# First two column-pair blocks of an up projection worked on form by form, with weight rings in the branches' memory and part of the sums on POOL

## The chip, the cores and the metric

The kernel runs on one core of a Trainium2 chip. The metric is the device time of one execution in microseconds (us), taken as the median of several runs. Engines are named as in the profile: PE is TensorE's matmuls and PEld its weight loads, DVE is VectorE, ACT is ScalarE, POOL is GpSimd, SP is the engine whose queue issues all DMAs of this kernel.

## The reference

One layer of a decoder trunk with two request groups: a prompt of 1024 tokens and 64 sample tokens (8 sequences of 8). All data is float32, the model width is 1024.

```python
mod = jax.nn.silu(c) @ p['w_ada'] + p['b_ada']
sh1, sc1, gt1, sh2, sc2, gt2 = jnp.split(mod, 6, axis=-1)
...
x = x + gt1[:, None] * (merged @ p['w_out'])
h = modulate(x, p['g_norm2'], sh2, sc2)
up = h @ p['w_up']
uc, new_ffn_conv = causal_dwconv(ffn_conv, up, p['ffn_conv_w'], p['ffn_conv_b'])
ua, ub = jnp.split(uc, 2, axis=-1)
x = x + gt2[:, None] * ((jax.nn.gelu(ua) * ub) @ p['w_down'])
```

Ahead of this stand a recurrent branch and a state-space branch ("the branches") that give `merged`; behind it a last norm. `modulate` is an RMS norm with a scale and a shift per channel that come from `mod`. `w_up` has 1024 rows and 6144 columns.

## The kernel before, in words

**Halves.** Activations lie with channels on the 128 partitions and tokens in columns. Tokens are cut into two halves: half 0 holds the 64 samples and 512 prompt tokens (576 columns), half 1 the other 512 prompt tokens. Float32 products are made from split operands: a value is rounded to the matmul's input format (`hi`, on ACT), the remainder `lo` is subtracted on DVE, and hi x hi, hi x lo and lo x hi are summed in PSUM. So every weight tile costs an ACT copy and a DVE subtraction (`wsplit` L167, `split_to` L240) before TensorE can use it.

**Stages.** `part1` (L1024) does the branches of one half, ending in the GLU strips and `merged`; `w_out` (L1106) does the output projection with the residual and adds up the squares of the new residual in `acc2`. Half 0 goes first. `h2a` (L1164), which turns half 0 into normalised forms, runs between the strips of half 1's GLU stage. Behind half 1's `w_out` the norm's reciprocal root `rB2` is made (`rstd_from` L349: a float32 matmul with ones, ACT root, DVE reciprocal), the pools of the branches are closed, new pools `forms` and `up` are opened, and `h2b` (L1189) and `up` (L1329) follow. Two down projections end the program.

**The modulation** `mod` is made in chunks of 512 columns: `adaB` (L1516) works on chunks 6 to 11 with split weights, eight pairs of matmuls (L269, L270) each, a few at every tick of the branches' strips of half 1.

**The up projection** treats the two halves of the tokens and two groups of weight columns as a 2 x 2 block product and uses seven products in place of eight (a Strassen-Winograd scheme). For each of 24 blocks of `w_up` four weight quarters A11, A12, A21, A22 are loaded (`quarters` L1242), and S1 = A21 + A22, S2 = S1 - A11, S3 = A11 - A21, S4 = A12 - S2 are made on DVE in place of the plain quarters. The activation side has seven "forms", made once, each in four tiles j = 0 to 3: B11 and B21 are half 0's; B22 is half 1's odd channel blocks, and with B12 its even ones, T1 = B12 - B11, T2 = B22 - T1, T3 = B22 - B12, T4 = B21 - T2. B11 and B21 come from `h2a`, the others from `h2b`. `prod` (L1225) is one product: four tiles of a form by three split terms; kinds "w" (two halves of 288 columns, 24 matmuls), "e" (512 columns, 12 matmuls) and "p" (two of 256, 24 matmuls).

`quad` (L1272) does one block in the order B11, [T4 of the block before], T1, T2, B21, B22, T3, and leaves T4 for the next block. It holds three PSUM tiles `b`, `e`, `a` of the ring `mm` (three buffers). Partial results are copied out by ACT (L1280, L1287, L1291) into the ring `cp` of four buffers, and `evac` (L1337) adds them on DVE into tiles of the ring `rx` of four. When both halves of a column tile are there, `finish` (L1353) runs the causal convolution: small copies on POOL (`fix` L1306), a scaled copy on ACT (L1320), two multiply-adds on DVE (L1322) for each half.

`h2b` loads half 1's residual (`x2B`, from DRAM, ring `rx`), multiplies by `rB2` on DVE (L1186), scales and shifts on ACT (L1187), loads half 0's raw values `hA` back (even blocks in ring `gl`, odd ones `C` in ring `cp`), makes the sums on DVE (L1207, L1212, L1213, L1217) and splits each tile (`split_form`: ACT L1147, DVE L1148).

**Order.** The program is written in one thread; a list scheduler lays it out per engine by priority, which is program order unless a `high_priority` block lifts it. Each engine, and SP's queue of DMAs, then runs its instructions strictly in that order. A tile of a ring is written only after its previous user has finished.

Of the kernel before, what the change touches and what calls it, by code (L numbers as in the profile page):

```python
# [8 lines left out]
F32 = mybir.dt.float32  # L9
# [42 lines left out]
def _body(ctx, nc, tc, a):  # L52
# [11 lines left out]
    wp, tp, ph = pool("w", 2), pool("tmp", 2), pool("part1")  # L64
    two = False
# [290 lines left out]
    def rstd_of(pr, name, tag="rstd", out=None):  # L356
        n = pr.shape[1]
        sd = rg("sd")[:, :n]
# [336 lines left out]
    us16 = ph.tile([128, 16, 16], F32, name="us16")  # L695
    ys16 = ph.tile([128, 16, 16], F32, name="ys16")
# [327 lines left out]
    def part1(half, L, X, during_glu, ahead=None):  # L1024
# [36 lines left out]
        drain(s5g)  # L1061
        during_glu()
# [43 lines left out]
    def w_out(half, merged):  # L1106
        acc2 = new_acc(f"acc2{half}")
# [76 lines left out]
    def norm_raw(dst, x, rstd, kb, t=None):  # L1184
        t = rg("nt")[:, :512] if t is None else t
        V.tensor_mul(t, x, rstd)  # L1186
        S.activation(dst, t, AF.Identity, scale=gmod["g2"][:, kb, 0:1], bias=modT[:, 24 + kb, 0:1])  # L1187

    def h2b():  # L1189

        def load(k, tag, w, n):
            t = tmp(tag, [128, w], n, bufs=4)[:, :576]
            nc.sync.dma_start(t, h2d[k])
            return t

        def nb2(dst, k):
            t = tmp("rx", [128, 656], "x2B", bufs=4)[:, :512]
            nc.sync.dma_start(t, x2d[1][k * 128:(k + 1) * 128])
            norm_raw(dst, t, rB2, k, tmp("xc", [128, 632], "nt", bufs=3)[:, :512])

        A, ST, C = [], [], []
# [12 lines left out]
        for j in range(4):  # L1214
            C.append(load(2 * j + 1, "cp", 576, "hA2"))
            split_form(form("T2", j), A[j])
            V.tensor_sub(C[j], C[j], A[j])  # L1217
        for j in range(4):
            split_form(form("B22", j), ST[j][:, 1])
        for j in range(4):  # L1220
            split_form(form("T3", j), ST[j][:, 0])
        for j in range(4):
            split_form(form("T4", j), C[j])

    def prod(acc, kind, wt, n, start=False, stop=False):  # L1225
        hi, lo = [x.rearrange("p (j c) -> p j c", c=128) for x in wt]
        for j in range(4):
            X = F[n, j]
            for i, (y, r) in enumerate(((hi, 0), (hi, 1), (lo, 0))):
                f = dict(start=start and j + i == 0, stop=stop and j == 3 and i == 2, skip_group_check=True)  # L1230
                w, x = y[:, j], X[:, r]
                if kind == "e":
                    T_.matmul(acc[:, 0], w, x, **f)  # L1233
# [8 lines left out]
    def quarters(w):  # L1242

        def new(n):
            return tmp("wr", [128, 512], n, bufs=WR)

        def load(q):
            t = new(f"wr{q}")
            nc.sync.dma_start(t, w[q])
            return t  # L1250

        def out(x):
            with tc.high_priority(offset=300):
                hi = tmp("wh", [128, 512], "wh", F32R, bufs=3)
                lo = tmp("wl", [128, 512], "wl", F32R, bufs=3)
                split_to(hi, lo, x)
            return hi, lo

        with tc.high_priority(offset=300):
            a11, a21, a22 = load(0), load(2), load(3)  # L1260
            s1 = new("s1")
            V.tensor_add(s1, a21, a22)
            s2 = new("s2")
            V.tensor_sub(s2, s1, a11)
            V.tensor_sub(a21, a11, a21)
            a12 = load(1)
            s4 = new("s4")
            V.tensor_sub(s4, a12, s2)
# [426 lines left out]
```

## Time and profile before

| | |
|---|---|
| median of 3 runs | 1776.75 us (1776.21 to 1778.32) |
| profiled execution | 1774.74 us |
| its span, first to last instruction | 1773.0 us |
| mean granted TensorE clock | 0.983 |
| instructions | 29389 |
| PE, PEld busy | 1693.0 us, 1533.8 us |
| DVE, ACT, POOL busy | 1243.4 us, 919.0 us, 187.3 us |

Times in a profile count from the first instruction. A granted clock of 1.00 is TensorE's higher level (2.4 GHz), 0.50 the lower (1.2 GHz). A wait row names the waiting engine, tile and line, and what released it.

### The profile page before, as it was taken

The page shows a single profiled execution, that of the slowest core. Times are in us where ns is not written, and L with a number is a line of the kernel's source. Part 1 is how long each engine was busy: PE and PEld are TensorE (multiplying, and loading weights), DVE is VectorE, ACT ScalarE, POOL GpSimd, SP SyncE. Part 2 cuts the span into 40 slices and gives each one's busy share as a digit, 9 for nine tenths or more (in the row PEclk, how much of TensorE's full clock was granted, in tenths as well). Part 3 has the DMA queues.
Part 4 walks back from the last instruction along what each step waited for, and adds up shares of the span by engine and source line. Part 5 has one row for each costly group of instructions (what it writes and reads, how often), then busy time and mean ns, then how long its engine had stood idle before and what let it go on. Part 6 is the DMA issues. An engine that isn't in the chain of part 4 may idle for free.

```text
span 1773.0 us, 29389 instructions
## 1 busy us (share of the span) xinstructions
PE 1693.0 (95%) x10538; PEld 1533.8 (87%) x10538; DVE 1243.4 (70%) x2645; ACT 919.0 (52%) x1616; POOL 187.3 (11%) x480
## 2 busy tenths in 40 slices
PE   7999999999999999999957999999999979999997
PEld 3899999899997877788746999999999978999887
DVE  8878688967746787756767777777777755435426
ACT  4657668435534588845445555545555435224224
POOL 0012110100000001000000222222222220000000
PEclk9999999999999999999978999999999999999999
DMA  8275344466646665446661222222222228546634
GB/s 308 74 236 168 99 119 127 126 187 194 205 125 203 213 182 153 151 125 193 196 205 32 78 76 77 80 79 75 79 75 79 73 64 289 166 130 191 197 95 136
DMA packets 151891, 250.87 MB, mean 142 GB/s; under 512 B 34112, under 2 KB 43328, under 8 KB 151744
## 3 DMA queue, kind: packets, MB, share of 16 engines
q1 hardware_dynamic: 151744, 248.99, 45.7%
q8 instruction: 83, 1.36, 0.3%
q14 instruction: 64, 0.52, 0.1%
HBM read 205.20 MB, written 43.73 MB: 140 GB/s over the span
## 4 chain that ended last, share of the span: by engine, by line
PE 65%; DVE 4%; DMA 4%; ACT 2%; issue 1%; POOL 0%; POOLq 0%; SPq 0%; DVEq 0%; ACTq 0%
PE mm L222 16%; PE b L1237 13%; PE mm L220 9%; PE e L1233 7%; PE mm L1415 7%; PE a L1237 4%; PE b L1240 4%; DMA al<-act 2%; PE pg L957 1%; DMA xB<-x 1%; PE sada L270 1%; PE sada L269 1%; DMA tgb<-tg 0%; DVE wlo L175 0%; PE sx L713 0%
## 5 line engine op out<-in xcount | busy, mean ns | idle before, releaser
L174 ACT ACTIVATE whi<-raw 128x512 fp32r<-128x512 f32 x310 | 194.5, 628 | 320.6 <-PE mm L222 104.5
L175 DVE TENSOR_TENSOR wlo<-raw,whi 128x512 fp32r<-128x512 f32 x310 | 213.1, 688 | 207.0 <-ACT whi L174 180.6
L220 PE MATMUL mm<-h1A,whi 128*128 128x288 f32 x1024 | 184.5, 299 | 0.0
L222 PE MATMUL mm<-h1B,whi 128*128 128x512 f32 x512 | 160.2, 393 | 0.0
L220 PEld LDWEIGHTS mm<-h1A,whi 128*128 128x128 f32 x1024 | 152.3, 190 | 0.2
L1237 PE MATMUL b<-T,wh 128*128 128x288 f32 x768 | 134.9, 298 | 14.5 <-ACT t L1280 13.2
L1237 PEld LDWEIGHTS b<-T,wh 128*128 128x128 f32 x768 | 115.7, 190 | 17.0 <-ACT t L1280 13.4
L241 ACT ACTIVATE wh<-wr 128x512 fp32r<-128x512 f32 x96 | 60.5, 630 | 113.8 <-PE b L1237 43.0
L222 PEld LDWEIGHTS mm<-h1B,whi 128*128 128x128 f32 x512 | 95.5, 188 | 23.7
L220 PE MATMUL mm<-h1A,wlo 128*128 128x288 f32 x512 | 111.0, 298 | 2.0 <-DVE wlo L175 2.0
L222 PE MATMUL mm<-h1B,wlo 128*128 128x512 f32 x256 | 100.7, 393 | 0.7 <-DVE wlo L175 0.7
L1322 DVE SCALAR_TENSOR_TENSOR uc<-up,vec,uc 128x624 f32<-128x624 f32 (+1 forms) x96 | 76.2, 815 | 30.6 <-ACT uc L1320 29.5
L1322 DVE SCALAR_TENSOR_TENSOR gl<-up,vec,gl 128x624 f32<-128x624 f32 (+1 forms) x96 | 75.5, 807 | 28.4 <-ACT gl L1320 27.6
L220 PE MATMUL mm<-act,whi 128*128 128x288 f32 x512 | 90.3, 297 | 1.6 <-ACT act L1147 1.1
L242 DVE TENSOR_TENSOR wl<-wr,wh 128x512 fp32r<-128x512 f32 x96 | 65.9, 686 | 34.7 <-ACT wh L241 34.2
L220 PEld LDWEIGHTS mm<-h1A,wlo 128*128 128x128 f32 x512 | 83.1, 190 | 2.3 <-DVE wlo L175 2.3
L1237 PE MATMUL b<-B,wh 128*128 128x288 f32 x384 | 68.3, 300 | 16.1 <-ACT wh L241 16.1
L1237 PE MATMUL b<-T,wl 128*128 128x288 f32 x384 | 82.9, 297 | 0.0
L1415 PE MATMUL mm<-act,whi 128*128 128x512 f32 (+1 forms) x304 | 82.7, 359 | 0.0
L220 PEld LDWEIGHTS mm<-act,whi 128*128 128x128 f32 x512 | 75.5, 189 | 2.8 <-DVE act L1148 1.4
L1237 PEld LDWEIGHTS b<-B,wh 128*128 128x128 f32 x384 | 57.6, 193 | 16.9 <-ACT wh L241 16.9
L241 ACT ACTIVATE wh<-s 128x512 fp32r<-128x512 f32 x72 | 45.0, 625 | 50.9 <-PE b L1237 42.6
(441 smaller groups left out, 4347.7 us busy)
## 6 DMA issues: line engine op xcount, KB each, us to landing
raw<-w_in SPq DMA_DIRECT2D x128, 256.0 KB, 2.8
raw<-w_down SPq DMA_DIRECT2D x105, 256.0 KB, 2.8
wr<-w_up SPq DMA_DIRECT2D x96, 256.0 KB, 2.7
raw<-w_ada SPq DMA_DIRECT2D x64, 256.0 KB, 3.0
act<-uc SPq DMA_DIRECT2D x48, 256.0 KB, 2.1
araw<-w_ada SPq DMA_DIRECT2D x16, 512.0 KB, 7.4
s5a<-s5d SPq DMA_DIRECT2D x16, 512.0 KB, 4.0
raw<-w_rgp SPq DMA_DIRECT2D x32, 256.0 KB, 2.7
```

What stands on the lines that cost most here:

```text
L174: S.activation(hi, raw, AF.Copy)
L175: V.tensor_sub(lo, raw, hi.bitcast(F32))
L220: T_.matmul(T[m][:, h, :288], y[:, k, c], x[:, r, h * 288:(h + 1) * 288], **f)
L222: T_.matmul(T[0][:, m, tok], y[:, k, c], x[:, r, tok], **f)
L241: S.activation(hi, src, AF.Copy)
L242: V.tensor_sub(lo, src, hi.bitcast(F32))
L269: T_.matmul(sa[:18], csr[:, kb], hi, start=kb == 0, stop=False)
L1233: T_.matmul(acc[:, 0], w, x, **f)
L1237: T_.matmul(acc[:, h, :288], w, x[:, h * 288:(h + 1) * 288], **f)
L1240: T_.matmul(acc[:, h, o:o + 256], w, x[:, h * 256:(h + 1) * 256], **f)
L1322: V.scalar_tensor_tensor(dst, t[:, k:k + n], fw[:, k, m:m + 1], dst, op0=OP.mult, op1=OP.add)
L1415: T_.matmul(T[:, m, tok], y[:, k, c], act[kb][:, r, tok], start=kb + n == 0, stop=kb == 23 and n == 2, skip_group_check=True)
```

## The change

It touches four things.

*Memory.* The tiles of the branches that are done early go into a pool `branches` on the other side of SBUF; `lead_weights`, called in `part1` of half 1 after the state-space branch has been drained and ahead of the GLU strips, closes it and puts the rings `wr`, `wh`, `wl` of the up projection's weights there. It loads the first block's four quarters at once and makes their sums on POOL.

*The norm.* The last two squares of `w_out` are not added by DVE; the norm's matmul takes three tiles. `rB2` is made inside `up_lead`.

*The forms.* `h2b` makes B22 first, then T1, T2, T3, T4. The subtractions of T3 and T4 go to POOL (`G`). T4 is made in `hA`'s own tile; the odd blocks come in the ring `xc` of three, as does the residual; the ring `cp` is left alone.

*The lead.* For the first two blocks (`w_up[0]` and `w_up[12]`, the two parts of one column pair) the products go form by form. The last modulation chunk is taken out of `adaB` and made behind the norm's matmul from float32 operands without a split. From the third block on the order is that of before. T1's product is now added on top of B22's in one PSUM tile for these two blocks, so their T3 evacuation has a subtraction and an addition.

```diff
+    early = ctx.enter_context(ExitStack())
+    rp = early.enter_context(tc.tile_pool(name="branches", bufs=1, side="right"))
+    RIGHT = ("s5", "yT", "gw", "us16", "ys16")
...
-        return ph.tile(shape, dt, tag=tag, name=name, bufs=bufs)
+        return (rp if tag.startswith(RIGHT) else ph).tile(shape, dt, tag=tag, name=name, bufs=bufs)
...
-        return tp.tile(shape, dt, tag=tag, name=name, bufs=bufs)
+        return (rp if rp is not None and tag in ("xc", "h") else tp).tile(shape, dt, tag=tag, name=name, bufs=bufs)
...
         drain(s5g)
+        if not smp:
+            lead_weights()
         during_glu()
...
-                acc_sq(acc2, xo, m == 0)
+                if half == 1 and b == 3:
+                    last.append(rg("sq")[:, :512])
+                    S.activation(last[-1], xo, AF.Square)
+                else:
+                    acc_sq(acc2, xo, m == 0)
...
-        return acc2
+        return [acc2, *last]
...
         def nb2(dst, k):
-            t = tmp("rx", [128, 656], "x2B", bufs=4)[:, :512]
+            t = tmp("xc", [128, 632], "x2B", bufs=3)[:, :512]
             nc.sync.dma_start(t, x2d[1][k * 128:(k + 1) * 128])
...
         for j in range(4):
-            A.append(load(2 * j, "gl", 632, "hA1"))
             ST.append(slot512(4 + j, f"h2B{j}"))
+            nb2(ST[j][:, 1], 2 * j + 1)
+            split_form(form("B22", j), ST[j][:, 1])
+        for j in range(4):
+            A.append(load("gl", 2 * j, 4))
+        for j in range(4):
             nb2(ST[j][:, 0], 2 * j)
-            t = tmp("wr", [128, 512], "t1f", bufs=WR)
-            V.tensor_sub(t, ST[j][:, 0], A[j][:, 32:544])
-            split_form(form("T1", j), t)
+            V.tensor_sub(A[j][:, 32:544], ST[j][:, 0], A[j][:, 32:544])
+            split_form(form("T1", j), A[j][:, 32:544])
+            G.tensor_sub(ST[j][:, 0], ST[j][:, 1], ST[j][:, 0])
         for j in range(4):
-            t3, b22 = ST[j][:, 0], ST[j][:, 1]
-            nb2(b22, 2 * j + 1)
-            V.tensor_sub(t3, b22, t3)
-            V.tensor_add(A[j][:, 32:544], t3, A[j][:, 32:544])
+            V.tensor_sub(A[j][:, 32:544], ST[j][:, 1], A[j][:, 32:544])
+            split_form(form("T2", j), A[j])
         for j in range(4):
-            C.append(load(2 * j + 1, "cp", 576, "hA2"))
-            split_form(form("T2", j), A[j])
-            V.tensor_sub(C[j], C[j], A[j])
-        for j in range(4):
-            split_form(form("B22", j), ST[j][:, 1])
+            c = load("xc", 2 * j + 1, 3)
+            G.tensor_sub(A[j], c, A[j])
         for j in range(4):
             split_form(form("T3", j), ST[j][:, 0])
         for j in range(4):
-            split_form(form("T4", j), C[j])
+            split_form(form("T4", j), A[j])
...
+        def sums(self, eng):
+            t = self.t
+            t["S1"] = wt("wr", "S1", F32, WR)
+            eng.tensor_add(t["S1"], t["A21"], t["A22"])
+            t["S2"] = wt("wr", "S2", F32, WR)
+            eng.tensor_sub(t["S2"], t["S1"], t["A11"])
+            eng.tensor_sub(t["A21"], t["A11"], t["A21"])
+            t["S3"] = t.pop("A21")
+            t["S4"] = wt("wr", "S4", F32, WR)
+            eng.tensor_sub(t["S4"], t["A12"], t["S2"])
...
+    def lead_weights():
+        nonlocal rp, uw
+        early.close()
+        rp = None
+        uw = early.enter_context(tc.tile_pool(name="upw", bufs=1, side="right", reuse_waits="tile"))
+        lead.append(Blocks(a["w_up"][0]))
+        lead[0].load("A11", "A21", "A22", "A12")
+        lead[0].sums(G)
...
+                elif e is not None:
+                    V.tensor_sub(o, y, z)
+                    V.tensor_add(o, o, e)
...
+    def up_lead():
+        nonlocal rB2
+        gl = {}
+        Q = [Quad(q, evac_up(0, i, gl)) for i, q in enumerate(lead)]
+        for i in range(2):
+            if i == 1:
+                x = slot512(2, "wx")
+                Q.append(Quad(Blocks(a["w_up"][12], (("A11", x[:, 0]), ("A12", x[:, 1]))), evac_up(0, 1, gl)))
+                Q[1].q.load("A11", "A12")
+            Q[i].p1()
+            Q[i].p2()
+        rB2 = slot(3, "rstdB2", F32)[:, 0, :512]
+        rstd_from(acc2, 512, "rstdB2", out=rB2)
+        e = mm("e")
+        ada_tail()
+        h2b()
+        Q[0].p3_first(e[:, 0])
+        with tc.high_priority(offset=300):
+            Q[1].q.load("A21", "A22")
+            Q[1].q.sums(G)
+        Q[1].p3_first(e[:, 1])
+        for q in Q:
+            q.p5_last()
+        Q[0].p6()
+        Q[0].c12()
+        Q[0].p7()
+        Q[0].p4()
+        Q[1].p6()
+        Q[1].c12()
+        Q[1].p7()
+        return Q[1]
+
+    def ada_tail():
+        sa = psum("ms", [128, 512], "sada")
+        for kp in range(4):
+            x = one(f"T3_{kp}", [128, 2, 512], "araw", F32)
+            nc.sync.dma_start(x, a["w_ada"][kp * 256:(kp + 1) * 256, 3584:4096].rearrange("(k p) c -> p k c", p=128))
+            for k in range(2):
+                T_.matmul(sa[:18], cs[:, 2 * kp + k], x[:, k], start=kp + k == 0, stop=kp + k == 4)
+        t = tmp("xc", [128, 632], "adat", bufs=3)
+        S.activation(t[:18, :512], sa[:18], AF.Copy)
+        ada_fin(44, 4, t)
...
-    adaB = ada_gen((6, 7, 8, 9, 10, 11), lambda: mm("sada")[:, 0],
+    adaB = ada_gen((6, 7, 8, 9, 10), lambda: mm("sada")[:, 0],
```

In the methods of `Quad`, p1 is the product of A11 with B11, p2 of A12 with B21, p3 of S4 with B22, p5 of S1 with T1, p6 of S2 with T2, p7 of S3 with T3, p4 of A22 with T4; `c12` is the evacuation that p3 and p5 end in.

## Rows read from the trace of the kernel before

**Rows 1.** First part of the page: busy us, share of the span, instructions

```profile
PE 1693.0 (95%) x10538; PEld 1533.8 (87%) x10538; DVE 1243.4 (70%) x2645; ACT 919.0 (52%) x1616; POOL 187.3 (11%) x480
```

**Rows 2.** Windows: us, busy of PE, PEld, DVE, ACT, POOL, PEclk, DMA share, GB/s

```profile
904.60:924.90 20.30, 1.21 (x4) 0.32 (x3) 16.84 (x23) 11.91 (x18) 0.46 (x1) 0.60 0.82 262
924.90:936.30 11.40, 11.40 (x60) 10.44 (x60) 11.40 (x19) 8.40 (x15) 0.00 (x0) 0.82 0.44 154
936.30:949.50 13.20, 0.03 (x2) 0.01 (x1) 12.85 (x22) 4.80 (x9) 0.00 (x0) 0.61 0.08 20
949.50:960.00 10.50, 10.50 (x61) 9.96 (x62) 6.64 (x10) 5.98 (x9) 2.18 (x8) 0.83 0.14 29
960.00:981.20 21.20, 21.20 (x146) 20.12 (x145) 14.33 (x22) 11.38 (x18) 2.96 (x12) 1.00 0.17 49
```

**Rows 3.** Waits of TensorE, 880 to 965: us in total, times, longest

```profile
PE b L1237 <- ACT wh L241: 16.1, 1, 16.1
PE b L1237 <- ACT t L1280: 13.2, 1, 13.2
```

**Rows 4.** The chain that ended last, products: start us, us, engine, tile, line

```profile
924.88 5.46 PE b L1237 x24
...
972.53 3.20 PE a L1237 x24
975.73 2.79 PE e L1233 x12
978.52 2.84 PE b L1240 x24
```

**Rows 5.** A window of the branches (columns as in 2), readers of tile h

```profile
772.00:800.00 28.00, 28.00 (x126) 23.17 (x125) 10.67 (x17) 7.52 (x13) 0.00 (x0) 1.00 0.48 139
...
L1006 DVE TENSOR_TENSOR gy<-gy,h x16: 666/686/693, 212.1 to 771.5; 128x512 f32<-128x512 f32 x16
```

**Rows 6.** Timeline of a chunk's pair, its window, fp32 matmuls at the start

```profile
736.18 0.39 PE L269 MATMUL sada<-adahl,csr 128*18 128x512 f32 x1
736.40 0.39 PE L270 MATMUL sada<-adahl,csr 128*18 128x512 f32 x1
...
720.00:740.00 20.00, 20.00 (x91) 15.23 (x90) 16.71 (x27) 17.80 (x31) 0.00 (x0) 1.00 0.58 184
...
19.77 3.63 PE L305 MATMUL sada<-araw,cs 128*18 128x256 f32 x16
```

**Rows 7.** Timeline of the norm's chain: start us, us, engine, line, operation

```profile
908.85 0.69 ACT L359 ACTIVATE sd<-prs,epst 128x512 f32<-128x512 f32 x1 [0.76 <-PE prs L353]
909.57 3.35 DVE L364 RECIPROCAL rstdB<-sd 128x512 f32<-128x512 f32 x1 [1.98 <-ACT sd L359]
...
913.68 0.81 ACT L1187 ACTIVATE h2B<-nt,modT,gm_g 128x512 f32<-128x512 f32 x1 [4.15 <-DVE nt L1186]
...
915.25 0.63 ACT L1147 ACTIVATE T<-t1f 128x512 fp32r<-128x512 f32 x1 [0.76 <-DVE t1f L1207]
```

**Rows 8.** VectorE while the forms are made: window, timeline, group

```profile
912.90:951.50 38.60, 13.45 (x68) 12.48 (x69) 36.89 (x60) 22.43 (x36) 1.14 (x2) 0.63 0.42 135
...
943.18 2.49 DVE L1148 TENSOR_TENSOR B<-h2B,B 128x512 fp32r<-128x512 f32 x4
...
L1217 DVE TENSOR_TENSOR hA<-hA,hA 128x576 f32<-128x576 f32 x4 | 3.0, 751 | 0.0
```

**Rows 9.** POOL beside VectorE: per line ns min/median/max, then timeline

```profile
L1369 DVE TENSOR_TENSOR uc<-uc,gl x48: 675/684/692, 981.7 to 1458.8; 128x512 f32<-128x512 f32 x48
...
L1367 POOL TENSOR_TENSOR cs<-uc,gl x24: 832/1317/1969, 981.3 to 1457.7; 128x64 f32<-128x64 f32 x24
...
1206.42 0.82 DVE L1322 SCALAR_TENSOR_TENSOR uc<-up,vec,uc 128x512 f32<-128x512 f32 x1
...
1238.30 0.74 DVE L1322 SCALAR_TENSOR_TENSOR uc<-up,vec,uc 128x512 f32<-128x512 f32 x1
```

**Rows 10.** VectorE in the GLU stage, timeline

```profile
843.97 0.69 DVE L1079 SCALAR_TENSOR_TENSOR q<-tgb,q 128x512 f32<-128x512 f32 x1 [2.96 <-DMA tgb<-tg]
```

More of the change, by code (lines that the diff above doesn't have):

```diff
@@ L694, in _body @@
     quarter = const.tile([128, 1], F32, name="quarter")
-    us16 = ph.tile([128, 16, 16], F32, name="us16")
-    ys16 = ph.tile([128, 16, 16], F32, name="ys16")
+    us16 = one("us16", [128, 16, 16], "us16")
+    ys16 = one("ys16", [128, 16, 16], "ys16")
     x2d = [dp.tile([1024, 512], F32, name=f"x2d{h}") for h in range(2)]
@@ L1106, in w_out @@
     def w_out(half, merged):
-        acc2 = new_acc(f"acc2{half}")
+        acc2, last = new_acc(f"acc2{half}"), []
         for b in range(4):
@@ L1240, in prod, with __init__, load, take @@
                             T_.matmul(acc[:, h, o:o + 256], w, x[:, h * 256:(h + 1) * 256], **f)
[L1242 to L1252, printed above, removed]
+    class Blocks:
+        def __init__(self, w, own=()):
+            self.w, self.t = w, dict(own)
+        def load(self, *names):
+            for n in names:
+                t = self.t.setdefault(n, None)
+                if t is None:
+                    t = self.t[n] = wt("wr", f"w{n}", F32, WR)
+                nc.sync.dma_start(t, self.w[{"A11": 0, "A12": 1, "A21": 2, "A22": 3}[n]])
+        def sums(self, eng):
[8 more added lines that the diff above has]
+            eng.tensor_sub(t["S4"], t["A12"], t["S2"])
+        def take(self, n):
@@ new lines, in blocks_of, with product, __init__, cp @@
+            q.load("A11", "A21", "A22", "A12")
+            q.sums(V)
+        return q
+    def product(q, acc, kind, n, x, **f):
+        prod(acc, kind, q.take(n), x, **f)
+    class Quad:
+        def __init__(self, q, evac):
+            self.q, self.evac, self.p3_ = q, evac, None
+        def cp(self, dst, src):
+            with tc.high_priority(offset=400):
+                S.activation(dst, src, AF.Copy)
+        def p1(self):
+            self.b = mm("b")
+            product(self.q, self.b, "w", "A11", "B11", start=True, stop=True)
+            self.t1 = tmp("cp", [128, 576], "t1", bufs=4)
+            self.cp(halves(self.t1), self.b[:, :, :288])
+        def p2(self):
+            a_ = mm("a")
+            product(self.q, a_, "w", "A12", "B21", start=True, stop=True)
+            self.evac(0, 0, a_[:, :, :288], halves(self.t1))
+        def p3_first(self, e):
+            self.e = e
+            product(self.q, e, "e", "S4", "B22", start=True, stop=True)
+            self.p3_ = tmp("cp", [128, 576], "p3", bufs=4)[:, :512]
+            self.cp(self.p3_, e)
+        def p5_last(self):
+            product(self.q, self.e, "e", "S1", "T1", stop=True)
+        def c12(self):
+            self.evac(0, 1, self.e, self.u2)
+        def p5(self):
+            self.e = mm("e")[:, 0]
+            product(self.q, self.e, "e", "S1", "T1", start=True, stop=True)
+            self.p5_ = tmp("cp", [128, 576], "p5", bufs=4)[:, :512]
+            self.cp(self.p5_, self.e)
+        def p6(self):
+            product(self.q, self.b, "w", "S2", "T2", stop=True)
+            self.u2 = tmp("cp", [128, 576], "u2", bufs=4)[:, :512]
+            self.cp(halves(self.u2), pmid(self.b))
+        def p3(self):
+            product(self.q, self.e, "e", "S4", "B22", stop=True)
+            self.c12()
+        def p7(self):
+            product(self.q, self.b, "p", "S3", "T3", stop=True)
+            if self.p3_ is None:
+                self.evac(1, 1, pmid(self.b), halves(self.p5_))
+            else:
+                self.evac(1, 1, pmid(self.b), halves(self.p3_), halves(self.e))
+        def p4(self):
+            product(self.q, self.b, "w", "A22", "T4", stop=True)
+            self.evac(1, 0, self.b[:, :, :288], None)
@@ L1351, in up @@
-        pend()
+                q = Quad(blocks_of(a["w_up"][12 * part + b]), evac_up(b, part, gl))
+                q.p1()
+                pend.p4()
+                q.p5()
+                q.p6()
+                q.p2()
+                q.p3()
+                q.p7()
+                pend = q
+        pend.p4()
     def finish(i, raw, part, m, gl, k):
@@ L1533, in _body @@
     tp = pool("up", 2)
-    h2b()
+    rB2 = None
     up()
@@ L1538, in _body @@
     phase.close()
+    early.close()
     pairs.close()
```

107 lines of the change are left out of this document (34 added, 73 removed).

## The prediction

> **What bounds the kernel now.** The page's first part says TensorE: it is busy 95% of the span, no other engine over 70% [rows 1]. So a change pays where TensorE stands idle or where it takes matmuls off TensorE. The windows around the start of the up projection show where that is [rows 2]: from the end of the second half's output projection (904.6 us) TensorE works 1.21 us of 20.30, then a burst of 11.40, then nothing for 13.20; only from 949.5 on is it busy without a break. The granted clock column shows 0.82 and 0.83 in the two bursts that follow the idle stretches, so part of each burst ran at the lower of its two levels (1.2 instead of 2.4 GHz).
>
> The waits name the two reasons [rows 3]. 16.1 us: the first product waits for the split of its first weight block, whose load is issued only after the new pools have opened. 13.2 us: the next product on the same PSUM tile waits for ScalarE's copy L1280; that copy needs a buffer of the ring `cp`, and `h2b` holds all four for its tiles `C` until T4 is split.
>
> Thirteen products (all seven of the first block, six of the second, up to its T3 product) end at 981.2, so they take 76.6 us from 904.6. At the high clock a product of 24 matmuls takes 3.20, an "e" product 2.79, a T3 product 2.84; the first product after the idle stretch took 5.46 [rows 4]. Work is therefore 7 x 3.20 + 4 x 2.79 + 2 x 2.84 = 39.2 us; 37 us of the 76.6 are waiting and low clock.
>
> **The change part by part.**
>
> *The lead.* Four products need only the first half's forms, which exist already: 4 x 3.20 = 12.8, so 904.6 to 917.4 if the weights are there. The first block's four loads and sums move into memory that the branches leave. In program order they stand before the GLU stage, and the last reader of that memory starts at 771.5. I let them run in 772 to 800, where VectorE is busy 10.67 of 28 us and DMA share is 0.48 [rows 5]: cost nothing; if that cover is gone they fall into the GLU stage (fourth rival). The second block's two loads wait for one merged tile that the output projection reads until its last strip, and land under the first two products, 6.4 us.
>
> *The norm.* Its matmul now sums three tiles and stands behind the four products. A 256-column fp32 record takes 3.63 / 16 = 0.227 [rows 6]; a 512-column fp32 matmul is two records of twice that, 0.91, so three take 2.7: 920.1. The two additions on VectorE that go (2 x 0.60) no longer lie on the path. Then, by the durations of the chain now [rows 7]: root 0.69, reciprocal 3.35, and with 0.1 for hand-over 924.2; multiply, shift and round 0.60 + 0.81 + 0.63: first B22 form at 926.2.
>
> *The modulation chunk.* Sixteen matmuls at 0.22 [rows 6] leave a stretch of the branches in which TensorE is busy 20.00 of 20 us [rows 6]: 16 x 0.22 = 3.5 us gained. Eight fp32 matmuls come back behind the norm, 8 x 0.91 = 7.3, from 920.1 to 927.4, under the chain of the norm, so free. Their four loads of 512 KB stand on SP's queue ahead of the residual's; 2 MB at the 262 GB/s of that window [rows 2] is 8 us, with the first three residual tiles 10.7 of the 19.6 us between 904.6 and 924.2, so hidden. The ring `xc` has three tiles, so later loads wait in SP's queue for a tile, and the loads behind them wait too; I take nothing, with 2 us as the bad end.
>
> *Forms.* From 924.2 VectorE is the engine to count: in the same work now it is busy 36.89 of 38.60 us [rows 8]. Back to back, 512 columns take (2.49 - 0.68) / 3 = 0.60, 576 columns about 0.67 [rows 8]. After: 28 operations of 512 columns (8 norm products; 4 each of T1's subtraction, T1's low part, T2's subtraction, B22's and T3's low parts) and 8 of 576 (the low parts of T2 and T4): 16.8 + 5.4 = 22.2. Added to that 8 weight splits (4.8), 5 evacuations (3.0, with the new extra subtraction in it) and about 8 convolution steps of finished tiles at 0.75 (6.0): 36.0, and 1.7 of bubbles as now: 961.9. One T3 product after that, 2.84: the thirteenth product ends at 964.7. TensorE alone would allow 904.6 + 39.2 + 2.7 + 7.3 = 953.8. So without contention 981.2 - 964.7 = 16.5 us are gained.
>
> *POOL.* The trace has no two-input POOL operation of 512 columns. Sixteen come: four in the branches, four early (second block, while VectorE waits for the norm) and eight beside the forms. What they cost VectorE is bounded so. From below nothing: 48 VectorE operations L1369 run next to POOL's 64-column multiplication and all take 675 to 692 ns [rows 9]. From above: POOL shuts VectorE out for all of its time. The 64-column operation lasts 832 to 1969 ns, median 1317 [rows 9]; for 512 columns 0.8 us (if length did not matter) to 10.5 (eight times the median). I take the nearest row: one VectorE operation that starts under that multiplication took 0.82 where its like takes 0.74 [rows 9], 0.08 more; times eight for the columns is 0.64, times eight operations 5.1 us on the path. The Trainium skill, page "SBUF — State Buffer", section "SBUF: two separate sides", says otherwise: a VectorE operation with two SBUF inputs and a reading POOL operation hold one port pair in turn, each for its whole length, the other stopped. By that rule the sum is -9.5 instead of -14.9 (second rival).
>
> *What queues behind.* POOL's sums stand ahead of the small copies of the first finished tiles; ScalarE's convolution copy waits for those, and through the ring `rx` the next evacuations: one or two sums, at most 2.6 us at 1.32, taken as nothing because VectorE's 36 us already fill that time. TensorE's bursts after 927 may run at the low level; a product then costs up to the 5.46 - 3.20 = 2.3 us seen now [rows 4], hidden while VectorE sets the pace, 2 us more if it is the last one.
>
> *The rest.* The other eleven column pairs run the same products in the same order; they are busy without a break now and stay so: nothing.
>
> **Sum.** -3.5 - 16.5 + 5.1 = -14.9 against the profiled execution's own 1774.74 (span 1773.0 and 1.7 around it): 1759.8. That execution lies 2.0 below the median of the runs, 1776.75, so the forecast is 1761.8, taken as 1762.
>
> **The rivals.** Differences under 0.2% (3.6 us) cannot be told from none here.
>
> 1. *Forecast*, 0.58: 1762; its own range 1756 to 1767.
>
> 2. *The port shuts VectorE out*, 0.14. Each of the eight POOL sums beside the forms stops it for a median 1.32: 8 x 1.32 = 10.5 instead of 5.1. -20.0 + 10.5 = -9.5: 1767. For it: nearly all of VectorE's work there has two SBUF inputs, and POOL's 64-column operations are stretched beside it. Against: the unstretched L1369. The Trainium skill, page "GPSIMD Engine Reference", section "3. Performance versus the Vector engine", gives 4497 ns for 2048 columns, by which one sum is an estimated 1.1 us and the eight 9.0; no run here shows it yet.
>
> 3. *Slower: POOL becomes the bound of the forms*, 0.08. T3 and T4 cannot be split before POOL has subtracted, and POOL takes them one by one. It decides when a sum costs the path more than 2.9 us: -20.0 + 8 x 2.95 = +3.6. At the upper bound, 10.5 each, it is +64: 1841; at 3.5 each it is +8: 1785. For it: the stretch to 1969 ns at 64 columns. Against: POOL stands idle otherwise, and VectorE waiting for it leaves it the port.
>
> 4. *The early work disturbs the GLU stage*, 0.09. There VectorE already waits 2.96 us for a DMA [rows 10]. If the 1 MB of weights or the POOL sums fall there, about that wait and its low-clock tail again, 5 us: 1767.
>
> 5. *TensorE-bound lead*, 0.08. If the norm's matmul is put ahead of the lead, as soon as the squares are there (907), VectorE starts 10 us earlier and 953.8 is reached: -27.4 - 3.5: 1746.
>
> 6. *It does not do what it says*, 0.03. If the early weights still wait for a tile that is released late, the first product waits its 16 us as now, and only the `cp` wait goes, mostly eaten by POOL: within 0.2%.
>
> **How the numbers follow.** Range 1749 to 1773: below it most of the fifth case, above it the third and sixth and the worse ends of the second and fourth. Faster by over 0.2%: cases 1, 2, 4, 5 less 0.03 for their bad ends, 0.86. Within: 0.06. Slower: 0.08.
>
> **What would show it.** In the profile after: no idle TensorE between 904 and 917 at granted clock 1.00; the chunk's fp32 matmuls before the first "e" product; no wait for the `cp` copy; VectorE nearly full from 924 to 960; the thirteenth product ending some 65 us after the output projection (964.7 + 5.1 - 904.6). VectorE operations of 512 columns at a pitch of over 1 us beside POOL's would show the second rival, TensorE waiting long on a split that waits for POOL the third. A gap in the GLU stage wider than now shows the fourth. I am wrong if the stretch from 904.6 to the thirteenth product stays over 73 us.

## The result and the profile after

The kernel after the change takes 1767.01 us (median, 1765.94 to 1769.02), the one before 1777.53 in the same session: a ratio of 0.9943, 95% interval 0.9925 to 0.9960. The forecast was 1762 us, a gain of 14.9 us; 10.5 were gained. (Ratios here and below are of undisturbed executions alone; in E11 the profiled one took 5095.7 us and is left out.)

"The stretch" below runs from the end of the second half's output projection to the end of the thirteenth product. The page's first part, the windows of the stretch (us, busy of PE, PEld, DVE, ACT, POOL, PEclk, DMA share, GB/s) and TensorE's waits from 895 to 972, which answer to [rows 1 to 3]:

```profile
PE 1707.3 (97%) x10542; PEld 1536.3 (87%) x10542; DVE 1246.5 (71%) x2621; ACT 913.9 (52%) x1608; POOL 228.6 (13%) x496
```

```profile
900.06:916.40 16.34, 15.57 (x103) 13.65 (x103) 6.02 (x7) 6.53 (x10) 2.68 (x8) 1.00 0.36 120
916.40:928.07 11.67, 7.42 (x22) 1.76 (x21) 5.24 (x9) 3.10 (x6) 1.14 (x4) 0.94 0.80 276
928.07:950.00 21.93, 15.86 (x45) 10.50 (x46) 20.64 (x25) 15.14 (x25) 8.75 (x6) 0.73 0.47 135
950.00:971.95 21.95, 20.12 (x127) 18.06 (x126) 21.95 (x30) 11.30 (x18) 6.17 (x8) 0.91 0.12 37
```

```profile
PE e L1242 <- DVE T L1158: 4.2, 3, 1.7
PE e L1242 <- ACT B L1157: 3.6, 1, 3.6
PE e L1242 <- ACT p L1302: 1.9, 2, 1.0
```

The waits of 16.1 and 13.2 us are gone. The lead runs at clock 1.00, as forecast; then come a second window in which VectorE is busy only 5.24 of 11.67 us, and two in which VectorE is full and TensorE's mean clock is 0.73 and 0.91. The output projection ends at 900.06, the thirteenth product, in the chain of work that ended last (start, us, engine, tile, line), at 971.95:

```profile
961.21 2.16 PE b L1249 x16
963.37 4.28 PE b L1246 x32
...
968.84 3.10 PE b L1249 x24
971.95 6.40 PE b L1246 x48
```

That is 71.9 us where the kernel before took 76.7 and the forecast was 65. From there to the down projection's start the two agree (483.1 and 483.2 us). Two places took the missing 7 us. First, the timelines of VectorE, ScalarE and TensorE around the norm's root (start, us, engine, line, operation, idle before it and what ended it):

```profile
914.63 3.35 DVE L368 RECIPROCAL rstdB<-rstdB 128x512 f32<-128x512 f32 x1 [1.78 <-ACT rstdB L363]
...
924.52 0.20 DVE L330 TENSOR_TENSOR modT<-adap,vec 128x36 f32<-128x36 f32 x1 [5.34 <-PE adap L328]
924.75 0.19 DVE L331 TENSOR_TENSOR modT<-modT,adap 128x36 f32<-128x36 f32 x1
925.25 1.34 DVE L1195 TENSOR_TENSOR x2B<-x2B,rstdB 128x512 f32<-128x512 f32 x2 [0.30 <-DMA x2B<-x2d]
```

```profile
912.61 1.28 ACT L363 ACT_TABLE_LOAD   x1
...
916.35 7.04 PE L1450 MATMUL sada<-araw,cs 128*18 128x512 f32 x16
924.07 0.42 PE L328 MATMUL adap<-vec,adat 18*128 18x18 f32 x4 [0.68 <-ACT adat L1452]
928.07 1.52 PE L1242 MATMUL e<-B,wh 128*128 128x512 f32 x2 [3.58 <-ACT B L1157]
```

The reciprocal ends at 917.98, the first norm product starts at 925.25. Between them VectorE stands for 5.34 us at L330, an addition of 36 columns that belongs to the modulation chunk: VectorE runs its queue in order, L330 needs the chunk's transposes, these its copy, and that its eight matmuls (16 records). At the same time SP's queue is late (DMA issues, and the piece of the chain of work that ended last):

```profile
911.25 1.97 SPq L1448 DMA_DIRECT2D araw<-w_ada  x4
913.26 0.93 SPq L1204 DMA_DIRECT2D hA<-h2d  x2
919.22 0.33 SPq L1262 DMA_DIRECT2D wA<-w_up  x1
919.59 0.91 SPq L1204 DMA_DIRECT2D hA<-h2d  x2
920.54 4.33 SPq L1209 DMA_DIRECT2D x2B<-x2d  x3
```

```profile
920.54 4.68 DMA x2B<-x2d
```

A weight load of the third block waits about 5 us for a tile of its ring, and the residual tiles `x2B` behind it are issued only at 920.54. The first lands at 925.22, 0.3 us after VectorE's two additions have ended, so both queues were late by nearly the same time, and the chain that ended last runs through the tile.

Second, VectorE's operations beside POOL's sums, grouped by shape, 925 to 967 (busy us, mean ns), POOL's own (ns min/median/max), and one pair from the two timelines:

```profile
L1224 DVE TENSOR_TENSOR hA<-h2B,hA 128x512 f32<-128x512 f32 x4 | 5.0, 1256 | 0.0
L1158 DVE TENSOR_TENSOR T<-hA,T 128x512 fp32r<-128x512 f32 x4 | 5.0, 1250 | 0.0
...
L1220 DVE TENSOR_TENSOR hA<-h2B,hA 128x512 f32<-128x512 f32 x4 | 2.6, 682 | 0.0
```

```profile
L1222 POOL TENSOR_TENSOR h2B<-h2B x4: 1275/1684/1722, 933.9 to 944.0; 128x512 f32<-128x512 f32 x4
L1228 POOL TENSOR_TENSOR hA<-hA x4: 1422/1794/1852, 945.6 to 956.4; 128x576 f32<-128x576 f32 x4
```

```profile
952.11 1.80 POOL L1228 TENSOR_TENSOR hA<-hA 128x576 f32<-128x576 f32 x1 [1.30 <-DVE T L1158]
952.55 1.90 DVE L1224 TENSOR_TENSOR hA<-h2B,hA 128x512 f32<-128x512 f32 x1
```

Eight VectorE operations, one for each POOL sum, take 1.56 to 1.90 us where the others of their size take 0.68; together they take 14.28 us, which is 14.28 - 8 x 0.68 = 8.84 us too much. (A group's mean near 1250 ns mixes operations of both kinds.)

### The profile page after: what moved, and what is told of

Same layout as the page of the kernel before. It is cut to its first block, busy times and chain, and to the rows that moved or that the text cites. A ratio compares the mean times of both kernels' runs of the same rounds, so it can differ in the third digit from the quotient of the medians.

```text
span 1767.2 us, 29386 instructions
## 1 busy us (share of the span) xinstructions
PE 1707.3 (97%) x10542; PEld 1536.3 (87%) x10542; DVE 1246.5 (71%) x2621; ACT 913.9 (52%) x1608; POOL 228.6 (13%) x496
## 4 chain that ended last, share of the span: by engine, by line
PE 68%; DVE 6%; DMA 4%; ACT 2%; issue 1%; SPq 0%; POOL 0%; POOLq 0%; DVEq 0%; ACTq 0%
PE mm L226 15%; PE b L1246 13%; PE mm L224 13%; PE e L1242 7%; PE mm L1533 7%; PE a L1246 4%; PE b L1249 4%; DMA al<-act 2%; DVE wlo L179 1%; DMA xB<-x 1%; PE pg L961 1%; PE pv L787 1%; PE sada L274 1%; PE sada L273 1%; PE sx L717 0%
## 5 line engine op out<-in xcount | busy, mean ns | idle before, releaser
L245 ACT ACTIVATE wh<-wA 128x512 fp32r<-128x512 f32 x94 | 59.2, 630 | 110.3 <-PE b L1246 42.0
L246 DVE TENSOR_TENSOR wl<-wA,wh 128x512 fp32r<-128x512 f32 x94 | 66.5, 708 | 26.6 <-ACT wh L245 26.1
L245 ACT ACTIVATE wh<-S 128x512 fp32r<-128x512 f32 x72 | 45.0, 625 | 53.8 <-PE b L1246 41.4
L224 PE MATMUL mm<-act,w 128*128 128x288 f32 x384 | 56.8, 303 | 13.3 <-ACT act L1157 11.7
L1242 PE MATMUL e<-T,wh 128*128 128x512 f32 x192 | 63.3, 409 | 5.2 <-DVE T L1158 4.2
```

The lines of the kernel that those rows point to most:

```text
L224: T_.matmul(T[m][:, h, :288], y[:, k, c], x[:, r, h * 288:(h + 1) * 288], **f)
L245: S.activation(hi, src, AF.Copy)
L246: V.tensor_sub(lo, src, hi.bitcast(F32))
L1242: T_.matmul(acc, w, x, **f)
```

## The experiments

All are edits of the kernel after the change. The table holds the median in us, the ratio to the kernel before with its interval, and three lengths of the profiled execution: the second half's branches (first matmul on `h1B`, near 530, to the output projection's end), and, counted from there, the start of the first product of the forms (the first "e" product, in the kernel before that of T1, in the others that of B22) and the thirteenth product's end. The intervals of E1 to E6 all overlap that of the kernel after: in the time alone none of them can be told from it, and what they show is in the three lengths.

| kernel | median | ratio | branches | first e | 13th |
|---|---|---|---|---|---|
| before | 1777.53 | 1 | 374.9 | 25.6 | 76.7 |
| after | 1767.01 | 0.9943 [0.9925, 0.9960] | 369.5 | 28.0 | 71.9 |
| e10 after, again | 1767.18 | 0.9949 [0.9935, 0.9963] | 371.1 | 27.9 | 71.8 |
| e1 chunk back | 1765.07 | 0.9934 [0.9919, 0.9950] | 373.9 | 21.9 | 65.8 |
| e2 finish late | 1766.76 | 0.9943 [0.9927, 0.9958] | 371.1 | 24.0 | 71.6 |
| e3 sums on VectorE | 1764.18 | 0.9930 [0.9915, 0.9946] | 370.8 | 28.4 | 68.3 |
| e4 = e2 + early loads | 1764.51 | 0.9927 [0.9909, 0.9946] | 371.8 | 25.4 | 66.7 |
| e5 = e1 + e3 | 1764.52 | 0.9932 [0.9920, 0.9944] | 374.5 | 21.9 | 61.9 |
| e6 = e4 + e3 | 1762.71 | 0.9927 [0.9913, 0.9941] | 371.9 | 28.3 | 66.8 |
| e7 = e5 + early norm | 1758.68 | 0.9901 [0.9887, 0.9916] | 376.1 | 18.5 | 58.5 |
| e8 = e6 + early norm | 1755.22 | 0.9888 [0.9870, 0.9906] | 370.8 | 22.6 | 60.8 |
| e12 e8, again | 1758.83 | 0.9907 [0.9891, 0.9924] | 371.9 | 22.6 | 61.0 |
| e9 = e8 + products first | 1754.06 | 0.9872 [0.9858, 0.9886] | 374.7 | 19.1 | 55.0 |

**E1, the chunk back in the branches.**

```diff
-    adaB = ada_gen((6, 7, 8, 9, 10), lambda: mm("sada")[:, 0],
+    adaB = ada_gen((6, 7, 8, 9, 10, 11), lambda: mm("sada")[:, 0],
-        ada_tail()
```

> The modulation's last chunk goes back into the pair of branches, as it stood before the change; the norm's chain, the two lead pairs and the sums on POOL stay as they are after the change. Theory A (the chunk's finish stands in front of the norm's products on VectorE): after the change the first product of the norm starts 7.3 us behind the end of the reciprocal (917.98 to 925.25), because the adds of L330 wait 5.34 us for the transposes. Without the chunk it should start within 1 us of the reciprocal; the thirteenth product then ends some 65 us behind the output projection's end instead of 71.9, and the branches take 3.5 to 4.2 us more. The whole comes to some 3 us below the kernel after the change, 1763 to 1765 us, a ratio of 0.992 to the kernel before. Rival (the residual loads, issued at 920.5 behind a weight load that waits on the same queue, and the transfers after them are what the norm's products really wait for): the stretch stays at 70 to 72 us, and the time rises by the branches' 3.5 to 4.2 us to about 1771.

The stretch comes out as theory A has it. VectorE's timeline:

```profile
918.51 3.35 DVE L368 RECIPROCAL rstdB<-rstdB 128x512 f32<-128x512 f32 x1 [1.78 <-ACT rstdB L363]
922.99 1.93 DVE L1195 TENSOR_TENSOR x2B<-x2B,rstdB 128x512 f32<-128x512 f32 x3
```

The first norm product starts 1.1 us behind the reciprocal (an evacuation and a weight split stand between), and no longer waits for its tile. The stretch is 6.1 us shorter, the branches are 4.4 longer (2.8 against E10, the same kernel as after). So the moved chunk gave back on the path what it freed, and more. The edit takes the chunk's four loads out of SP's queue too, so it can't tell VectorE's queue from SP's; E2 and E4 do.

**E2, the chunk's finish behind the forms.**

```diff
-        ada_tail()
+        sa = ada_tail()
...
         Q[1].p7()
+        ada_last(sa)
```

`ada_last` holds the copy, the transposes and the adds that `ada_tail` ended with.

> The chunk's eight float32 matmuls stay behind the norm's; its copy, transposes and adds move to behind the last pair of forms of the second column block, where nothing waits for them at once. Theory A: the first product of the norm follows the reciprocal by under 1 us where its residual tile has landed; the stretch from the output projection's end to the thirteenth product falls from 71.9 us to about 65, the branches stay as short as after the change: about 1760 us, ratio 0.990. Rival (residual loads late by the load queue): the norm's product still starts 5 us or more behind the reciprocal, now behind its residual tile, the stretch stays at 70 us or more, and the time at about 1767; the next kernel, which issues those loads earlier, alone gains.

The rival holds in the stretch, 71.6 us, and in the time; its 5 us behind the reciprocal are 3.3. The adds are gone from VectorE's queue, yet the first norm product starts 2.05 us behind the last split, and the next tiles come late too (VectorE's waits, 915 to 965; a piece of the chain that ended last; SP's issues):

```profile
DVE x2B L1195 <- DMA x2B<-x2d: 3.2, 2, 2.0
```

```profile
912.11 7.84 DMA x2B<-x2d
```

```profile
918.03 0.33 SPq L1262 DMA_DIRECT2D wA<-w_up  x1
918.40 0.43 SPq L1204 DMA_DIRECT2D hA<-h2d  x1
921.61 0.32 SPq L1209 DMA_DIRECT2D x2B<-x2d  x1
```

The scheduler now issues the first three residual tiles at 912.11, ahead of the weight load but behind the chunk's four loads, and the first lands only 7.84 us later. The fourth is issued at 921.61, 3.6 us after the weight load that held the queue.

**E4, the residual loads early as well.**

```diff
-            nc.sync.dma_start(t, x2d[1][k * 128:(k + 1) * 128])
+            with tc.high_priority(offset=2000):
+                nc.sync.dma_start(t, x2d[1][k * 128:(k + 1) * 128])
```

> As the kernel before this one in the list (the chunk's finish behind the forms), and the residual loads of the norm are also issued earlier in the order of the load queue, ahead of the third block's weight load that waited 5 us for its tile. Theory A alone (VectorE's queue was the only cause): the same time as without the earlier loads, about 1760 us. Theory of both (once the adds are gone the residual tile ends the wait): 3 to 5 us faster than without the earlier loads, about 1760 us, where the other stays at 1764 to 1767. Rival (neither; TensorE's own lower clock and the products of the forms set the pace): both stay within 2 us of the kernel after the change.

The theory of both holds in the stretch: 66.7 us, 4.9 below E2. The median is only 2.3 us below E2's and 4.5 above the forecast. Now the chunk's loads stand behind the residual's, and TensorE waits 2.1 us for them. So the chunk's price is two queues: VectorE's, where its adds stood, and SP's, where its four loads and the weight loads stood ahead of the residual tiles. Taking it out of one shows the other.

**E3, the eight sums of the forms back on VectorE.**

```diff
-            G.tensor_sub(ST[j][:, 0], ST[j][:, 1], ST[j][:, 0])
+            V.tensor_sub(ST[j][:, 0], ST[j][:, 1], ST[j][:, 0])
...
-            G.tensor_sub(A[j], c, A[j])
+            V.tensor_sub(A[j], c, A[j])
```

> The eight subtractions of the norm's forms (T3 and T4 of the two pairs) go back from POOL to VectorE; nothing else differs from the kernel after the change. Theory (a POOL sum of 512 columns stops one VectorE operation for about 1.1 us: eight operations took 1.56 to 1.90 us where their kind takes 0.68): no VectorE operation of the forms is over 1 us, 8.8 us of stretched time go and 8 x 0.62 = 5.0 us of sums come, so the thirteenth product ends 68 us behind the output projection instead of 71.9 and the kernel takes about 1763 us. Rival (the offload pays as forecast: 8 x 0.64 us saved on VectorE): the stretch grows by some 5 us to 77 and the kernel takes about 1772 us.

68.3 us and 1764.18, as the first theory has it. The two groups at 1256 and 1250 ns, 924 to 966:

```profile
L1158 DVE TENSOR_TENSOR T<-hA,T 128x512 fp32r<-128x512 f32 x4 | 2.7, 684 | 0.0
...
L1224 DVE TENSOR_TENSOR hA<-h2B,hA 128x512 f32<-128x512 f32 x4 | 2.7, 688 | 0.0
```

The same edits cost and bring the same on top of E1:

**E5, both parts undone** (the diffs of E1 and E3 together).

> Both secondary parts undone together: the modulation's last chunk back in the branches and the eight sums of the forms back on VectorE. What is left of the change is the two lead pairs, the norm worked on form by form, and the lead's weight sums on POOL. Theory: the parts add. From the output projection's end to the down projection's start the kernel before took 559.8 us, after 555.1, with the chunk back 548.9, with the sums back 552.6; so here 548.9 - 2.5 = about 546.4, the branches of the second half as before (374 us), the whole about 1762.5 us, ratio 0.992. Rival (the two overlap: the forms are already fed by something else once either is gone): the stretch stays at 548 to 549 us and the time at 1765.

61.9 against E1's 65.8, 3.9 less: the two losses add. From the output projection's end to the down projection's start it takes 546.1 us (expected 546.4); the median, 1764.5, is 2 us above the forecast. What the lead, the early weights and the norm form by form bring by themselves is 76.7 - 61.9 = 14.8 us in the stretch, 13.7 to the down projection's start (559.8 before).

**E6, finish late, loads early, sums on VectorE** (the diffs of E2, E4 and E3).

> The chunk's finish behind the forms, the residual loads early, and the eight sums on VectorE. Theory: the branches keep the 3 to 5 us that the moved chunk freed (second half's branches 370 to 372 us against 374 to 375 with the chunk in them), and the stretch to the down projection's start falls to 550.5 - 2.5 = 548 us or less: about 1761 us, ratio 0.991. Rival (the chunk's matmuls, 7.04 us of TensorE in front of the forms' products, and its 1 MB of loads still cost there what they freed): the stretch 550 us or more, the time as with the chunk in the branches, 1762 to 1765.

The rival holds: 551.6 us to the down projection's start, 66.8 to the thirteenth product, no less than E4's 66.7, so here the sums on VectorE brought nothing. TensorE's timeline shows why:

```profile
921.05 8.74 PE L1452 MATMUL sada<-araw,cs 128*18 128x512 f32 x16 [3.30 <-DMA araw<-w_ada]
929.72 0.73 PE L1243 MATMUL e<-B,wh 128*128 128x512 f32 x2
```

The chunk's matmuls wait for their loads and then hold back the first product of the forms.

**E7 and E8, the norm's matmul behind the first lead product** (on top of E5 and of E6).

```diff
             Q[i].p1()
+            if i == 0:
+                rB2 = slot(3, "rstdB2", F32)[:, 0, :512]
+                rstd_from(acc2, 512, "rstdB2", out=rB2)
             Q[i].p2()
-        rB2 = slot(3, "rstdB2", F32)[:, 0, :512]
-        rstd_from(acc2, 512, "rstdB2", out=rB2)
```

> Chunk in the branches, sums on VectorE, and the norm's three matmuls behind the first of the four lead products instead of behind the third. Theory (VectorE is the stretch's bound, and the lead delays its start): the root and the reciprocal end some 6 us earlier, 11 to 12 us behind the output projection's end instead of 18, and the first norm product follows at once; the lead's splits and evacuations (3 us of VectorE) now stand among the forms, so the thirteenth product and the down projection's start come 3 to 5 us earlier than in the kernel with both parts undone: about 1758 to 1759 us. Rival (the residual tiles, written by the output projection and loaded behind the weights, or TensorE with its four products come last): a gain under 1 us.

> As the last one, but with the chunk moved out of the branches, its finish behind the forms and the residual loads early. Theory: the branches 370 to 372 us and the earlier norm together, about 1756 us, the lowest of all. Rival (the chunk's 7 us of matmuls are now on the path, since the norm's chain ends before TensorE has done them): the first product of the forms waits for TensorE, the stretch is 3 us or more longer than in the kernel before it in the list, and the two times are within 1 us.

E7 goes as its theory says. The reciprocal ends 11.0 us behind the output projection (907.63), the stretch is 3.4 us below E5, the time 1758.68:

```profile
915.26 3.35 DVE L368 RECIPROCAL rstdB<-rstdB 128x512 f32<-128x512 f32 x1 [3.31 <-ACT rstdB L363]
```

E8's branches are 5.3 us shorter than E7's and its first median is 3.5 us lower; but its repeat, E12, has the ratio 0.9907 beside E7's 0.9901, so in the time the two can't be told apart, as its rival says. Its stretch is 2.3 us longer than E7's, since the first product waits for TensorE:

```profile
915.75 6.18 PE L1453 MATMUL sada<-araw,cs 128*18 128x512 f32 x14
921.87 0.73 PE L1243 MATMUL e<-B,wh 128*128 128x512 f32 x2
```

**E9, the first product ahead of the chunk's matmuls** (on top of E8).

```diff
-        Q[0].p3_first(e[:, 0])
+        with tc.high_priority(offset=300):
+            Q[0].p3_first(e[:, 0])
```

> As the kernel with the early norm and the chunk moved out (1755.2 us), but the first product of the forms (Q0's S4 by B22) is given priority over the chunk's float32 matmuls, so that these fall into the gaps of the forms' products. There the first such product starts 22.6 us behind the output projection's end, right behind 6.18 us of the chunk's matmuls, where the kernel with the chunk in the branches starts it at 18.5; the stretch to the down projection's start is 545.6 us against 542.8. Theory (TensorE held up by the chunk makes this difference): the first product at 18 to 19 us, the stretch near 543, the time about 1752 to 1753 us. Rival (the chunk's and the residual tiles' loads, issued together, make it): the stretch stays at 545 to 546 us and the time at 1755.

The first theory holds and the stretch goes beyond it: the first product starts at 19.1 us, the stretch is 55.0 us, 5.8 shorter than E8's, and 540.8 us pass to the down projection's start (expected near 543). TensorE's timeline and two windows:

```profile
919.87 1.89 PE L1454 MATMUL sada<-araw,cs 128*18 128x512 f32 x4
921.69 0.73 PE L1243 MATMUL e<-B,wh 128*128 128x512 f32 x2
922.26 0.39 PE L1243 MATMUL e<-B,wl 128*128 128x512 f32 x1
922.50 0.40 PE L1243 MATMUL e<-B,wh 128*128 128x512 f32 x1
922.82 1.03 PE L1454 MATMUL sada<-araw,cs 128*18 128x512 f32 x2
```

```profile
902.56:921.69 19.13, 19.13 (x111) 14.34 (x109) 12.50 (x15) 11.75 (x18) 5.22 (x8) 1.00 0.70 228
921.69:957.54 35.85, 32.93 (x177) 24.87 (x176) 34.86 (x56) 22.29 (x37) 2.26 (x5) 1.00 0.36 121
```

The chunk's matmuls now fill gaps, and VectorE, 34.86 of 35.85 us, is what is left. The stretch is also 3.5 us shorter than E7's, which has no chunk there, so the chunk's hold on TensorE is not all that the edit took away; what the rest is was not separated. From the thirteenth product to the down projection's start it takes 485.9 us, 2.8 more than in the kernel before, so a part is lost again. The median is 1 us below E8's first; the branches of this execution took 374.7.

**E10 to E12, the kernel after, E9 and E8 once more, unchanged.**

> The kernel after the change once more, beside the others: 1766 to 1767 us, the stretch from the output projection's end to the down projection's start 555 us and the second half's branches 369 to 371 us, as in its first profile; the first half of the down projection, whose code no run here changes, between 168.6 and 172.4 us, the bounds of the profiles so far, and not always at 172.4.

> The version with the first product of the forms ahead of the chunk's matmuls once more, beside the one without. In its first profile the branches of the second half took 374.7 us where the kernels with the chunk out of them took 369.5 to 371.9, though nothing there differs. Theory (variation between executions): this time 370 to 372 us, the stretch to the thirteenth product 55 us as before, and the median 3 to 5 us under that of the version without, near 1751. Rival (the loads issued earlier do delay the branches): 374 to 375 us again, and the two medians within 2 us, as in the last calls.

> The version with the early norm and the chunk's finish behind the forms once more, as the companion of the last: 1755 us, the branches 370 to 372 us, the thirteenth product 61 us behind the output projection's end, as in its first profile.

E10 repeats the profile after to 0.1 us in the stretch; its branches take 371.1 us where that profile has 369.5. The time of E8's kernel came out 3.8 us above the forecast, 1758.83, with the stretch as before. E11 has no profile of use, so it tells nothing of the branches; its other four runs lie at 1751.6 to 1755.0, ratio 0.9872 [0.9854, 0.9891] beside 0.9907 [0.9891, 0.9924] for E8's kernel on the same chip. So the version of E9 is faster than both kernels of this case, and by all signs than E8's, though those two intervals touch. Why E9's branches took 3 to 4 us more than E8's in the one profile stays open; what is seen there is a wait for a load of the branches (tile `s5a`) of 2.3 us where E8's profile has 0.6, and one of 1.5 us for a weight split that E8's has not, in code that is the same.

## Why the prediction was right, and where it was not

**Direction and place: right; the size, in part luck.** The two waits went, the rest of the up projection kept its time, and the gain is in the stretch and the branches where it was looked for. But the stretch gave 4.8 us where -16.5 + 5.1 = -11.4 was forecast, and at 71.9 us it came near the 73 at which the prediction called itself wrong. The measured 1767.0 is the number of the second and fourth rivals and the upper end of the forecast's own range, not its 1762. The sign named for the second rival is in the trace (1.56 to 1.90 us beside POOL), and the POOL term, 8.84, lies nearer to its 10.5 than to the forecast's 5.1; that the second rival's number fits to the microsecond is luck, since its sum has nothing for the chunk's 6.1. Point by point:

- *Branches, -3.5: right.* Four profiles with the chunk in them (before, E1, E5, E7) average 374.8 us, nine without it 371.5: 3.3, with a spread of 5 us among the nine.
- *The lead and its weights at no cost: right.* Three products of 3.20 without a gap. The first block's POOL sums start at 773.06, where TensorE is busy 28.00 of 28 us, and from 840 to 880 it is busy 38.27 of 40 us, 37.95 in the same window before; the fourth rival is out. The windows, two of after, then one of before:

```profile
772.00:800.00 28.00, 28.00 (x126) 23.17 (x125) 13.22 (x18) 7.24 (x12) 7.79 (x5) 1.00 0.54 171
840.00:880.00 40.00, 38.27 (x166) 30.28 (x165) 29.71 (x47) 18.62 (x31) 0.00 (x0) 1.00 0.66 204
...
840.00:880.00 40.00, 37.95 (x161) 30.77 (x160) 28.35 (x45) 18.48 (x32) 0.00 (x0) 0.96 0.65 204
```

- *The norm: right by errors that cancel.* The first B22 form was due 21.6 us behind the output projection; in E1 the product that reads it starts at 21.9. But the norm's matmul stands behind three lead products, not four, 3.2 us earlier; against that, between it and the root came ScalarE's copies for the lead and a load of the activation table of 1.28 us, which the kernel before had under a wait, and between the reciprocal and the first product an evacuation and a split.
- *"Under the chain of the norm, so free": this step failed.* It compared the chunk's matmuls with the norm's chain in time, and left out that the chunk ends in two additions on VectorE, ahead of the norm's products in an in-order queue, behind matmuls, a copy and transposes. What waits in SP's queue ("I take nothing, with 2 us as the bad end") failed too: it is the other half (E2, E4). Together they cost 6.1 us (E1). (The loads' transfer time, 10.7 us in the working, should read 11.0; nothing hangs on it.)
- *POOL, 5.1: mis-sized.* 8.84 us. The nearest row taken, 0.08 us for 64 columns, was an operation that met only the last 0.27 us of a POOL instruction. Nor did the unstretched L1369 speak against the rival: the same 64-column multiplication takes 0.33 us in the trace after, so in the median 1.32 of [rows 9] POOL was mostly the one that waited:

```profile
973.68 0.33 POOL L1485 TENSOR_TENSOR cs<-uc,gl 128x64 f32<-128x64 f32 x1
```

  E3 and E5 show what the move is worth: the eight sums cost 3.6 to 3.9 us more on POOL than on VectorE. This is the second rival's mechanism: each sum stopped one VectorE operation for 0.88 to 1.22 us. The Trainium skill says so in "SBUF — State Buffer", section "SBUF: two separate sides" (an exclusive lock for the whole instruction); this trace agrees. The Trainium skill's "GPSIMD Engine Reference", section "3. Performance versus the Vector engine", gave an estimate of 1.1 us for a sum by itself; alone it took 1.29 (773.06). That 8.84 / 8 is 1.10 as well is luck: a sum beside VectorE was 1.27 to 1.85 us long, and the stopped operation met a part of it.
- *The forms' 36 us: about 3 too long.* E5, without the chunk and with the sums on VectorE, should by the working have taken 60.1 + 8 x 0.60 = 64.9; it took 61.9. Of the eight convolution steps, 6.0 us, the first starts at 966.75 in the kernel after, behind the last form; against that, the working left out the third block's four weight sums on VectorE (L1267, L1269, L1270, L1273), 4 x 0.60 = 2.4 us. The first of them:

```profile
951.95 0.68 DVE L1267 TENSOR_TENSOR S<-wA,wA 128x512 f32<-128x512 f32 x1
```

The balance: 65.2 + 6.1 + 3.7 - 3.0 = 72.0 for the 71.9 measured. Its last term is what E5 left over, so it shows that the parts add, and no more. Outside the stretch a disagreement remains: the profiled executions differ by 5.7 us, the medians by 10.5. The one before, 1774.74, lies below all four runs of its kernel, and the one after, 1769.02, is the slowest of its four. The first half of the down projection (its first matmul to the last norm's), the same code everywhere, took 168.6 us in the profile before, 172.4 and 171.0 in the two after, 168.9 to 171.7 in the experiments: twelve profiles, all longer than the one before. Whether part of that is the change's doing was not settled. Of the medians' 10.5 us the traces tie 4.7 (to the down projection's start) and 3.3 (branches) to the change.

**The fifth rival,** 1746 with the norm ahead of the lead, was tried in part as E7 to E9, with the norm's matmul behind the first lead product: 1754 at best. Its 953.8 took TensorE for the bound; in E9 VectorE still is (34.86 of 35.85 us), and the stretch is 55.0 us against the rival's 49.2.

## What to carry to other kernels

When a step is moved into a wait, follow it to its last instruction on every queue: the expensive part of this chunk was first not its 7 us of matmuls but a 0.2 us addition at the head of VectorE's queue, and four loads on SP's; once these were out of the way, the matmuls showed too (E6, E8). A sum moved to POOL cost TensorE nothing where VectorE had time to spare (773 to 781); where VectorE was full, it stopped VectorE longer (1.10 us) than the sum would have taken there (0.60). And moving the norm's matmul two products forward, three lines, brought more (5.8 us, E5 to E7) than undoing the change's two secondary parts (some 2 us, after to E5, within the intervals).

## What was not expected of the hardware

A POOL sum of 512 columns takes 1.29 us alone (773.06). Beside VectorE the one that started ahead of VectorE's operation (933.88) took 1.27, and the three that started while one was running took 1.66 to 1.72, so either engine is stretched, whichever comes second; of the VectorE operations that overlap a sum, one alone is. And TensorE's granted clock was low where TensorE had gaps: after the change it idled 3.58 us ahead of the first "e" product and was granted 0.73 on average from 928 to 950, between its two levels, with eleven of that product's matmuls taking 5.39 us (twelve take 2.79 at the higher level); in E9, where the chunk's matmuls filled gaps, it stayed at 1.00, the higher level, from 902.6 to 957.5.
